# Convolution inputs and decay gates in whole float32, GpSimd out of the first block's splits, and modulation sums moved later

## The chip, the cores and the metric

The kernel runs on one NeuronCore of a Trainium2 chip. The metric is the device time of one execution in microseconds (us); lower is better. TensorE multiplies, VectorE (DVE) and ScalarE (ACT) do elementwise work, GpSimd (POOL) does elementwise work on SBUF, and SyncE (SP) issues most of the transfers.

## The reference, cut to what matters

Two transformer blocks over 256 tokens of width 1024, all in float32. The first block has chunked attention and a gated delta rule side by side, then a feed-forward layer; the second has retention, differential attention and a mixture of 32 experts. The change is in the first block:

```
u = rms_norm(h, mix_norm_gain);  proj = u @ w_in
aq, ak, av, dqkv, dgate, da, db = split(proj)
o_att = rms_norm(chunked_rel_attention(aq, ak, av))
dqkv = causal_short_conv(dqkv)               # 3 x 512 columns: q, k, v of the delta rule
log_decay = -exp(a_log) * softplus(da + dt_bias);  beta = sigmoid(db)
o_dn = rms_norm(gated_delta_rule(dq, dk, dv, log_decay, beta)) * silu(dgate)
h = h + concat(o_att, o_dn) @ w_out
h = h + square(relu(rms_norm(h) @ w_ff1)) @ w_ff2
```

The second block begins with `mod = silu(c) @ w_ada + b_ada`, six vectors of 1024 that scale and shift its norms.

## The kernel before, in words

Most products are made of three passes. Weights come from HBM as float32 tiles `raw` (128 x 2048, 1 MB, a ring of four buffers). `split` cuts a 128 x 1024 piece in two: ScalarE casts it to a rounded high part `hi` (L144), and VectorE or GpSimd subtracts to get the low part `lo` (L145). The numbers in the tuple `POOL` are the splits, counted in the order in which they are written, that GpSimd gets. The activations are kept in the same way as `xh` and `xl`. `gemm_t` then does hi times xh, hi times xl and lo times xh, with the weights stationary and 256 columns moving (L168 to L170); `gemm_b` has the activations stationary and 512 columns moving (L197 to L199). These operands are fp32r; the other products of the kernel have whole float32 operands.

The first block is written as pieces of work. First come the decay gates (`ab_load`, `ab_gemm`, L374 to L376), `conv(1)` (the keys: one `gemm_t` of 512 columns, then the four-tap convolution on VectorE, L325, and SiLU, L328 and L329), `decays`, `l2(1)` and `gram`. Then `level(l, t)` for l = 0 to 6 and two halves t solves the triangular system of the delta rule step by step: GpSimd masks (B, L509), TensorE multiplies (w, L520), ScalarE copies (Ws, L522), TensorE multiplies (u, L527), VectorE subtracts (U, L528). The remaining work is the list `todo`: the convolutions of queries and values, the attention products `qk_gemm`, `v_gemm`, the `head`s, the gate product `gate_gemm`. `ORDER` holds for each entry of the list the level behind which it is written. Behind level 7 comes `scan` (a chain of small products, L533, each waiting for the one before), and at the end `dn_out` and the output product.

A scheduler moves instructions on each engine within what the data allow, by the order in which they are written, so work that is written later fills waits of earlier work. What each engine gets is fixed when the program is built, and each engine works strictly in that order.

`fill` advances the modulation sums: six generators `ada(i)` of four steps each. A step loads 1 MB of `w_ada_2` into the same ring `raw` and adds two 128 x 1024 products on VectorE (L836). `FILL` says how many steps are taken where: five in the first block and 16 in the feed-forward layer; `fill(99)` in the second block takes the last three. The end of the kernel, the experts, streams their weights from HBM.

Of the kernel before, what the change touches and what calls it, by code (L numbers as in the profile page):

```python
# [23 lines left out]
PI_LO = 3.1415925  # L24
FILL = ((0, 0, 0, 0, 0, 0, 1, 2, 2, 0), (1, 1, 1, 1, 0, 1, 1, 1, 1, 1, 1, 1, 1, 1, 1, 2))
NRAW = 4
CHECK = 7
NRAW2B = 2
NRAW2C = 1
ORDER = (1, 2, 2, 6, 6, 6, 7.1, 6.9, 7.9, 6, 6, 6, 8, 8, 8, 8, 8, 8, 8, 8, 8)  # L30
POOL = (1, 5, 8, 9, 11, 13, 14, 21, 24, 25, 30, 31, 32, 33, 36, 37, 38, 40, 42, 48, 60, 83, 104, 106, 117, 140, 144, 152, 155, 158, 186, 187)
TI = 1
# [59 lines left out]
class Build:  # L92
# [66 lines left out]
    def gemm_t(self, W, c0, xt, bank=None):  # L159
# [11 lines left out]
        return [b.rearrange("p (c s) -> p c s", c=2) for b in banks]  # L171

    def gemm_b(self, W, c0, xt, outer=0, halves=(0, 1), bank=None, hook=None):


        nc = self.nc
        xh, xl = xt
        banks = [(bank or self.acc)() for _ in range(2)]
        ps = self.pieces(W, c0, halves)
        def steps():  # L180
            n = 4 * len(halves) - outer
            for _ in range(n):
                p = next(ps)
                for t in range(2):
                    yield t, p
            rest = list(ps)
            for t in range(2):
                for i, p in enumerate(rest):
                    if t == 1 and hook:
                        hook(i, banks)  # L190
                    yield t, p

        k0, k1 = halves[0] * 4, halves[-1] * 4 + 3
        for t, (k, hi, lo) in steps():
            ts = slice(t * 128, (t + 1) * 128)
            o = banks[t]
            nc.tensor.matmul(o, xh[:, k, ts], hi, start=(k == k0), stop=False)  # L197
# [42 lines left out]

    def part_T(self, src, t, k0, gains, xt, bank=None):
# [11 lines left out]
        f = self.t(self.sm, [128, 4, 128], "pf")  # L253
# [38 lines left out]
    def block1(self, x, ctx):  # L292
        nc, d = self.nc, self.d
        T = self.t
# [4 lines left out]
        ss = T(self.sm, [128, 2, 2], "ss")  # L299
        xt = self.xt()  # L300
        for half in range(2):
            for t in range(2):
                self.part_T(x[:, t, half * 512:(half + 1) * 512], t, 4 * half, mix, xt)
        cb = T(p1, [128, 8 * 128], "cb")
# [6 lines left out]
        def conv(s):  # L311
            banks = self.gemm_t(W, 1536 + 512 * s, xt)
            ct = T(p1, [128, 4, 256], f"cT{s}")
# [51 lines left out]
        def ab_load():  # L365
            rawab = T(self.raw, [128, 8, 128], "raw")
            nc.sync.dma_start(rawab, W[:, 3464:3592].rearrange("(k p) c -> p k c", p=128))
            return self.split(rawab.rearrange("p k c -> p (k c)"))

        def ab_gemm(hi, lo):  # L370
            pab = self.mis()
            for k in range(8):
                w = slice(k * 128, (k + 1) * 128)
                nc.tensor.matmul(pab[:, :256], hi[:, w], xt[0][:, k, :], start=(k == 0), stop=False)  # L374
                nc.tensor.matmul(pab[:, :256], hi[:, w], xt[1][:, k, :], start=False, stop=False)
                nc.tensor.matmul(pab[:, :256], lo[:, w], xt[0][:, k, :], start=False, stop=(k == 7))  # L376
            abT = T(p1, [128, 256], "abT")
# [311 lines left out]
        nc.vector.tensor_scalar(rh, r, 0.5, None, op0=OP.mult)  # L689
        ab = ab_gemm(*ab)  # L690
        self.modulation()
# [13 lines left out]
        for t in range(2):  # L705
            gram(t)
        ct = self.xt()
        todo = [lambda: conv(0), lambda: l2(0), lambda: [intra(t) for t in range(2)],
                lambda: qk_gemm(0), lambda: self.fill(FILL[0][7]), lambda: qk_gemm(1), lambda: self.fill(FILL[0][8]), v_gemm, qk_norm,
                lambda: conv(2), lambda: [values(t) for t in range(2)], lambda: self.fill(FILL[0][9])]  # L710
        todo += [lambda h=h: head(h) for h in range(8)]
        todo += [gate_gemm]

        def steps(l):
            for a, i in sorted((a, i) for i, a in enumerate(ORDER)):
                if l <= a < l + 1:
                    todo[i]()

        for l in range(7):
            for t in range(2):  # L720
                level(l, t)
            self.fill(FILL[0][l])
            steps(l)
# [5 lines left out]
        steps(8)  # L729
        dn_out()  # L730
        for t in range(2):
            self.part_T(odn[t], t, 4, gc, ct, self.acc)
        out = [self.gemm_b(d["w_out"][0], half * 512, ct, halves=(1,)) for half in range(2)]
        ra = att_rms()
# [14 lines left out]
    def ffn(self, x, zt, ss, ctx):  # L749
# [9 lines left out]
        def up(s):  # L759
            banks = self.gemm_t(d["w_ff1"][0], 512 * s, zt, bank=self.mis)  # L760
            self.fill(FILL[1][2 * s])
            zh = T(p2, [128, 2, 512], "zh", F32R)
# [11 lines left out]
        for s in range(8):  # L774
# [6 lines left out]
            for half in range(2):  # L781
# [3 lines left out]
                for kk in range(2):  # L785
                    pcs.append((half * 2 + kk, raw[:, kk, :]))
            self.fill(FILL[1][2 * s + 1])
            if s < 7:
# [129 lines left out]
    def block2(self, x, ss, inner, outer):  # L918
# [70 lines left out]
        for s in range(2):  # L989
            banks = self.gemm_b(W, 2048 + 512 * s, xt)  # L990
            for t in range(2):
                cs = slice(s * 512, (s + 1) * 512)
# [14 lines left out]
        dq.append(roped(3584, dqa[:, 4:8, :]))  # L1007
        dk = [roped(4096 + 512 * s, dka[:, 4 * s:4 * s + 4, :]) for s in range(2)]
        dv = tokens(5120, 2, "rv")
# [602 lines left out]
    def run(self):  # L1612
        x = self.setup()
        dense = ExitStack()
        self.sps, self.nsplit, self.total = [self.sp] * 3 + [self.pool("sp1", 1, ctx=dense, side="right")], 0, 0
        with ExitStack() as c:
            zt, ss = self.block1(x, c)
        dense.close()
        if self.stop <= 1:
# [59 lines left out]
```

## Time and profile before

| what | value |
|---|---|
| median of 3 runs | 1209.8 us (1206.2 to 1212.64) |
| the profiled execution | 1207.75 us, span 1205.9 us |
| mean granted TensorE clock | 0.974 of 2.4 GHz |
| busy over the span | TensorE 94%, VectorE 48%, ScalarE 34%, GpSimd 18% |
| first block | from 0 to about 226 us |
| feed-forward layer, second block up to the experts | about 226 to 410, 410 to 726 us |
| experts | about 726 us to the end |

The profile calls the engines PE, DVE, ACT, POOL and SP. A row of the timeline is one instruction or a run of like ones: start, duration, engine, line, output <- inputs, count; the bracket behind it is the idle time of the engine before it and what ended it. Matmuls overlap, so what one of them costs in a stream is the distance of two starts. A product with float32 operands on both sides stands in the trace as two records (a row of x2 is one such instruction).

### The profile page before, as it was taken

The numbers are of one execution on the slowest core, as the hardware profiler recorded it, in microseconds if no ns is written. First come the engines' busy times: TensorE is split into PE (matmuls) and PEld (weight loads), VectorE is DVE, ScalarE is ACT, GpSimd is POOL, SyncE is SP. The second block draws the span as 40 slices with busy tenths as digits, with TensorE's granted clock in tenths as the row PEclk, the third lists the DMA queues.
The fourth block names the chain that finished last, engine by engine and source line by source line (L and its number), as shares of the span: only waits on it lengthen the run. The fifth ranks groups of instructions, "written<-read, shape, count | busy, mean of one in ns | idle before, by whom it ended". The sixth has DMA issues, their size and how long they took to land. (4 is left out here: it accounts for less than half of the span.)

```text
span 1205.9 us, 16461 instructions
## 1 busy us (share of the span) xinstructions
PE 1130.5 (94%) x6638; PEld 810.5 (67%) x6639; DVE 576.6 (48%) x863; ACT 406.0 (34%) x692; POOL 220.6 (18%) x149
## 2 busy tenths in 40 slices
PE   6789799999999999999899989999999799999997
PEld 6768676899899798998899975434343344343443
DVE  5994845786666684788565652111111111120112
ACT  5534344545444445534654441111010011110112
POOL 2472641622010121532220210000000000000011
PEclk9989897999999999999999998999999899999999
DMA  8442531788686746657458585999999999999991
GB/s 300 140 139 72 175 113 51 281 301 283 231 298 240 263 154 185 199 162 258 140 151 292 191 283 217 419 418 415 419 417 415 417 418 415 417 418 416 416 402 62
DMA packets 95728, 331.67 MB, mean 275 GB/s; under 512 B 6528, under 2 KB 11280, under 8 KB 79648
## 3 DMA queue, kind: packets, MB, share of 16 engines
q1 hardware_dynamic: 93152, 327.70, 72.7%
q10 hardware_dynamic: 2448, 2.79, 0.7%
q8 instruction: 53, 0.87, 0.3%
q14 instruction: 27, 0.22, 0.0%
q0 software_dynamic: 48, 0.08, 0.0%
HBM read 329.50 MB, written 1.05 MB: 274 GB/s over the span
## 5 line engine op out<-in xcount | busy, mean ns | idle before, releaser
L144 ACT CAST hi<-raw 128x1024 fp32r<-128x1024 f32 x189 | 197.2, 1046 | 219.2 <-PE acc L169 88.0
L145 DVE TENSOR_TENSOR lo<-raw,hi 128x1024 fp32r<-128x1024 f32 x157 | 210.5, 1350 | 92.6 <-ACT hi L144 90.3
L169 PE MATMUL acc<-xl,hi 128*128 128x256 f32 x544 | 155.2, 285 | 0.9 <-DVE xl L938 0.8
L168 PE MATMUL acc<-xh,hi 128*128 128x256 f32 x544 | 155.8, 287 | 0.0
L170 PE MATMUL acc<-xh,lo 128*128 128x256 f32 x544 | 154.5, 284 | 0.3 <-POOL lo L145 0.3
L169 PEld LDWEIGHTS acc<-xl,hi 128*128 128x128 f32 x544 | 105.0, 193 | 1.4 <-DVE xl L938 1.3
L168 PEld LDWEIGHTS acc<-xh,hi 128*128 128x128 f32 x544 | 105.1, 193 | 0.2
L170 PEld LDWEIGHTS acc<-xh,lo 128*128 128x128 f32 x544 | 104.6, 192 | 0.6 <-POOL lo L145 0.5
L145 POOL TENSOR_TENSOR lo<-raw,hi 128x1024 fp32r<-128x1024 f32 x32 | 80.8, 2530 | 101.0 <-ACT hi L144 100.1
L1422 PE MATMUL mis<-raw,xh 128*64 128x512 f32 x328 | 98.3, 595 | 0.0
L197 PE MATMUL acc<-hi,xh 128*128 128x512 f32 x208 | 86.5, 417 | 0.0
L1413 POOL TENSOR_TENSOR early<-early,x 128x512 f32<-128x512 f32 x4 | 5.0, 1275 | 444.8 <-DVE early L1412 444.8
L198 PE MATMUL acc<-lo,xh 128*128 128x512 f32 x208 | 85.1, 409 | 0.0
L199 PE MATMUL acc<-hi,xl 128*128 128x512 f32 x208 | 84.9, 408 | 0.0
L1467 DVE TENSOR_TENSOR xh<-mis,xh 128x512 fp32r<-128x512 f32 x30 | 20.5, 691 | 115.1 <-ACT xh L1466 114.9
L168 PE MATMUL mis<-xh,hi 128*128 128x256 f32 x256 | 72.6, 284 | 0.0
L170 PE MATMUL mis<-xh,lo 128*128 128x256 f32 x256 | 72.5, 283 | 0.0
L169 PE MATMUL mis<-xl,hi 128*128 128x256 f32 x256 | 72.5, 283 | 0.0
L1433 DVE SCALAR_TENSOR_TENSOR pf<-pf,mis 128x512 f32<-128x512 f32 x16 | 11.0, 688 | 119.6 <-ACT pf L1432 119.6
L836 DVE SCALAR_TENSOR_TENSOR ada<-raw,sc,ada 128x1024 f32<-128x1024 f32 x42 | 61.6, 1467 | 6.8 <-DMA raw<-in_w_ada 6.3
L1422 PE MATMUL mis<-early,xh 128*64 128x512 f32 x256 | 62.9, 595 | 0.0
L1422 PEld LDWEIGHTS mis<-raw,xh 128*64 128x64 f32 x328 | 29.6, 137 | 46.4 <-issue 45.2
(463 smaller groups left out, 2112.1 us busy)
## 6 DMA issues: line engine op xcount, KB each, us to landing
raw<-in_w_in SPq DMA_DIRECT2D x46, 1024.0 KB, 5.4
raw<-in_w_ff SPq DMA_DIRECT2D x32, 1024.0 KB, 5.9
raw<-in_w_exp_up SPq DMA_DIRECT2D x26, 1024.0 KB, 15.0
raw<-in_w_ada SPq DMA_DIRECT2D x24, 1024.0 KB, 6.3
early<-in_w_exp_gate SPq DMA_DIRECT2D x22, 1024.0 KB, 12.6
raw<-in_w_exp_gate SPq DMA_DIRECT2D x15, 1024.0 KB, 17.4
hi<-in_w_exp_up SPq DMA_DIRECT2D x26, 512.0 KB, 13.9
lo<-in_w_exp_up SPq DMA_DIRECT2D x26, 512.0 KB, 12.6
```

The lines of the kernel that those rows point to most:

```text
L144: nc.scalar.copy(hi, raw)
L145: (nc.gpsimd if self.total in POOL else nc.vector).tensor_sub(lo, raw, hi.bitcast(F32))
L168: nc.tensor.matmul(o, hi[:, w], xh[:, k, :], start=(k == 0 and cb % 2 == 0), stop=False, skip_group_check=True)
L169: nc.tensor.matmul(o, hi[:, w], xl[:, k, :], start=False, stop=False, skip_group_check=True)
L170: nc.tensor.matmul(o, lo[:, w], xh[:, k, :], start=False, stop=(k == 7), skip_group_check=True)
L197: nc.tensor.matmul(o, xh[:, k, ts], hi, start=(k == k0), stop=False)
L198: nc.tensor.matmul(o, xh[:, k, ts], lo, start=False, stop=False)
L199: nc.tensor.matmul(o, xl[:, k, ts], hi, start=False, stop=(k == k1))
L836: nc.vector.scalar_tensor_tensor(a, raw[:, kk, :], self.sc[:, k:k + 1], a, op0=OP.mult, op1=OP.add)
L1422: nc.tensor.matmul(o[i * 64:(i + 1) * 64, :], xg[:, k, j % 2 * 128 + i * 64:j % 2 * 128 + (i + 1) * 64], raws[i][kk // 2][:, kk % 2 * 512: ...
L1433: nc.vector.scalar_tensor_tensor(th, th, 1.0, pgt, op0=OP.add, op1=OP.mult)
L1467: nc.vector.tensor_sub(yp[:, 1, c, :], py[c], yp[:, 0, c, :].bitcast(F32))
```

## The change

Three edits and what follows from them. (1) `conv` and `ab_gemm` multiply `raw` by a new tile `xf`, the unrounded activations, in one float32 pass (`gemm_f`); 13 splits (12 of the three convolutions, one of the gates) fall away. (2) `POOL` no longer names a split of the first block: 15 of its 37 splits were GpSimd's, and all 24 that are left are VectorE's. Behind the first block it names the same splits as before, their numbers moved by 13. (3) The five steps of `fill` in the first block move to the second: behind each `gemm_b` of `tokens` and of the retention gates, and once ahead of `dk`. Besides, `ORDER` and a new tuple `OUTS` write the gate product ahead of `scan`, and `dn_out` and the output product's delta-rule half between the heads; the first block's hi and lo have three buffers each in place of four.

```
-FILL = ((0, 0, 0, 0, 0, 0, 1, 2, 2, 0), (1, 1, 1, 1, 0, 1, 1, 1, 1, 1, 1, 1, 1, 1, 1, 2))
+FILL = (1, 1, 1, 1, 0, 1, 1, 1, 1, 1, 1, 1, 1, 1, 1, 2)
-ORDER = (1, 2, 2, 6, 6, 6, 7.1, 6.9, 7.9, 6, 6, 6, 8, 8, 8, 8, 8, 8, 8, 8, 8)
-POOL = (1, 5, 8, 9, 11, 13, 14, 21, 24, 25, 30, 31, 32, 33, 36, 37, 38, 40, 42, 48, 60, 83, 104, 106, 117, 140, 144, 152, 155, 158, 186, 187)
+ORDER = (1, 2, 2, 6, 6, 6.8, 7.9, 6, 6.7, 8.1, 8.2, 8.3, 8.4, 8.6, 8.7, 8.9, 8.95, 6.6)
+OUTS = (8.5, 8.65, 8.8)
+POOL = (24, 25, 27, 29, 35, 47, 70, 91, 93, 104, 127, 131, 139, 142, 145, 173, 174)
...
+    def gemm_f(self, W, c0, xf):
...
+        banks = [self.acc() for _ in range(2)]
+        for half in range(2):
+            raw = self.t(self.raw, [128, 4, 512], "raw")
+            nc.sync.dma_start(raw, W[half * 512:(half + 1) * 512, c0:c0 + 512].rearrange("(k p) c -> p k c", p=128))
+            for kk in range(4):
+                k = half * 4 + kk
+                for cb in range(4):
+                    nc.tensor.matmul(banks[cb // 2][:, (cb % 2) * 256:(cb % 2 + 1) * 256], raw[:, kk, cb * 128:(cb + 1) * 128], xf[:, k, :],
+                                     start=(k == 0 and cb % 2 == 0), stop=(k == 7), skip_group_check=True)
...
         def conv(s):
-            banks = self.gemm_t(W, 1536 + 512 * s, xt)
+            banks = self.gemm_f(W, 1536 + 512 * s, xf)
...
             for k in range(8):
-                w = slice(k * 128, (k + 1) * 128)
-                nc.tensor.matmul(pab[:, :256], hi[:, w], xt[0][:, k, :], start=(k == 0), stop=False)
-                nc.tensor.matmul(pab[:, :256], hi[:, w], xt[1][:, k, :], start=False, stop=False)
-                nc.tensor.matmul(pab[:, :256], lo[:, w], xt[0][:, k, :], start=False, stop=(k == 7))
+                nc.tensor.matmul(pab[:, :256], raw[:, k, :], xf[:, k, :], start=(k == 0), stop=(k == 7))
...
         todo = [lambda: conv(0), lambda: l2(0), lambda: [intra(t) for t in range(2)],
-                lambda: qk_gemm(0), lambda: self.fill(FILL[0][7]), lambda: qk_gemm(1), lambda: self.fill(FILL[0][8]), v_gemm, qk_norm,
-                lambda: conv(2), lambda: [values(t) for t in range(2)], lambda: self.fill(FILL[0][9])]
+                lambda: qk_gemm(0), lambda: qk_gemm(1), v_gemm, qk_norm,
+                lambda: conv(2), lambda: [values(t) for t in range(2)]]
         todo += [lambda h=h: head(h) for h in range(8)]
         todo += [gate_gemm]
+        out = []
+
+        def dn_turn():
+            dn_out()
+            for t in range(2):
+                self.part_T(odn[t], t, 4, gc, ct, self.acc)
+
+        todo += [dn_turn] + [lambda half=half: out.append(self.gemm_b(d["w_out"][0], half * 512, ct, halves=(1,))) for half in range(2)]
...
             for s in range(n):
                 banks = self.gemm_b(W, c0 + 512 * s, xt)
+                self.fill()
```

Two places on VectorE and one on TensorE show how the order moves. On VectorE, between the two halves of the keys' squared sums (`ssd`) and their scaling (`qk`), stood before:

```order
L351 TENSOR_SCALAR ssd_88_441<-ssd_88_441 128x4
L836 SCALAR_TENSOR_TENSOR ada_962<-raw_963,sc_95,ada_962 128x1024
L318 TENSOR_TENSOR pre_675<-acc_556,rrow_178 128x2x256
L145 TENSOR_TENSOR lo_988<-raw_969,hi_987 128x1024
L351 TENSOR_SCALAR ssd_88_441<-ssd_88_441 128x4
L325 SCALAR_TENSOR_TENSOR cT_129_674<-pre_675,cw_224,cT_129_674 128x256
L359 TENSOR_TENSOR qk_93_461<-qk_93_461,rdd_87_440 128x512
L325 SCALAR_TENSOR_TENSOR cT_129_674<-pre_675,cw_224,cT_129_674 128x256 x4
```

and at the same place in the changed kernel stands:

```order
L367 TENSOR_SCALAR ssd_75_335<-ssd_75_335 128x4
L146 TENSOR_TENSOR lo_797<-raw_778,hi_796 128x1024
L146 TENSOR_TENSOR lo_815<-raw_812,hi_814 128x1024
L367 TENSOR_SCALAR ssd_75_335<-ssd_75_335 128x4
L375 TENSOR_TENSOR qk_80_355<-qk_80_355,rdd_74_334 128x512
L334 TENSOR_TENSOR pre_489<-acc_450,rrow_168 128x2x256
L460 SCALAR_TENSOR_TENSOR L_296<-mis_378,beta_140,L_296 128x128 x4
```

The modulation product is gone, a second low part stands in its place, and the convolution of the queries (`cT`) has moved behind the gram product (L460, before L447). On VectorE in levels 1 and 2 (the four subtractions from U), before:

```order
L528 TENSOR_TENSOR U_507<-U_507,mis_535 128x128x2
L325 SCALAR_TENSOR_TENSOR cT_129_674<-pre_689,cw_224,cT_129_674 128x256
L145 TENSOR_TENSOR lo_1022<-raw_1003,hi_1021 128x1024
L836 SCALAR_TENSOR_TENSOR ada_962<-raw_1047,sc_95,ada_962 128x1024
L528 TENSOR_TENSOR U_518<-U_518,mis_550 128x128x2
L329 SCALAR_TENSOR_TENSOR cT_129_674<-sq_700,cT_129_674 128x512
L836 SCALAR_TENSOR_TENSOR ada_962<-raw_1047,sc_95,ada_962 128x1024
L836 SCALAR_TENSOR_TENSOR ada_962<-raw_1051,sc_95,ada_962 128x1024
L528 TENSOR_TENSOR U_507<-U_507,mis_718 128x64x4
L836 SCALAR_TENSOR_TENSOR ada_962<-raw_1051,sc_95,ada_962 128x1024
L528 TENSOR_TENSOR U_518<-U_518,mis_739 128x64x4
```

and now:

```order
L541 TENSOR_TENSOR U_401<-U_401,mis_429 128x128x2
L341 SCALAR_TENSOR_TENSOR cT_108_488<-pre_489,cw_198,cT_108_488 128x256
L341 SCALAR_TENSOR_TENSOR cT_108_488<-pre_503,cw_198,cT_108_488 128x256 x2
L345 SCALAR_TENSOR_TENSOR cT_108_488<-sq_500,cT_108_488 128x512
L341 SCALAR_TENSOR_TENSOR cT_108_488<-pre_503,cw_198,cT_108_488 128x256 x3
L541 TENSOR_TENSOR U_412<-U_412,mis_444 128x128x2
L341 SCALAR_TENSOR_TENSOR cT_108_488<-pre_503,cw_198,cT_108_488 128x256
L146 TENSOR_TENSOR lo_831<-raw_812,hi_830 128x1024
L345 SCALAR_TENSOR_TENSOR cT_108_488<-sq_514,cT_108_488 128x512
L541 TENSOR_TENSOR U_401<-U_401,mis_532 128x64x4
L541 TENSOR_TENSOR U_412<-U_412,mis_553 128x64x4
```

Four modulation products between the subtractions are gone, and convolution steps stand there that were done earlier before. On TensorE at the scan (L533, now L546), before:

```order
L533 MATMUL mis_1422<-vb_1287,U_507 128x128 x4
L198 MATMUL acc_1692<-lo_1697,xh_106 128x512
L199 MATMUL acc_1692<-hi_1696,xl_107 128x512
L197 MATMUL acc_1693<-hi_1696,xh_106 128x512
L198 MATMUL acc_1693<-lo_1697,xh_106 128x512
L199 MATMUL acc_1693<-hi_1696,xl_107 128x512
L197 MATMUL acc_1692<-hi_1696,xh_106 128x512
L533 MATMUL mis_1429<-D_1421,kt_147 128x128 x4
L198 MATMUL acc_1692<-lo_1697,xh_106 128x512
```

and now:

```order
L214 MATMUL acc_1094<-hi_1147,xl_104 128x512
L601 MATMUL mis_1171<-ca_84,qk_179_846 128x128 x4
L601 MATMUL mis_1178<-ca_84,qk_181_851 128x128 x4
L601 MATMUL mis_1186<-ca_84,qk_195_926 128x128 x4
L601 MATMUL mis_1193<-ca_84,qk_197_931 128x128 x4
L546 MATMUL mis_1200<-vb_1084,U_401 128x128 x4
L546 MATMUL mis_1207<-D_1199,kt_141 128x128 x4
L546 MATMUL mis_1214<-s_248_1206,cT_56_243 128x128 x4
L546 MATMUL mis_1222<-Ws_1213,U_412 128x128 x4
L546 MATMUL mis_1228<-D_1199,LT_297 128x128 x4
```

The products that stood between the scan's steps now stand ahead of it, and nothing stands between the steps.

## Rows read from the trace of the kernel before

**Rows 1.** The page: mean GB/s that the transfers moved, in 40 equal slices.

```profile
GB/s 300 140 139 72 175 113 51 281 301 283 231 298 240 263 154 185 199 162 258 140 151 292 191 283 217 419 418 415 419 417 415 417 418 415 417 418 416 416 402 62
```

**Rows 2.** The page's costliest groups: out<-in xcount, busy us, mean ns, idle before.

```profile
L145 DVE TENSOR_TENSOR lo<-raw,hi 128x1024 fp32r<-128x1024 f32 x157 | 210.5, 1350 | 92.6 <-ACT hi L144 90.3
...
L145 POOL TENSOR_TENSOR lo<-raw,hi 128x1024 fp32r<-128x1024 f32 x32 | 80.8, 2530 | 101.0 <-ACT hi L144 100.1
...
L836 DVE SCALAR_TENSOR_TENSOR ada<-raw,sc,ada 128x1024 f32<-128x1024 f32 x42 | 61.6, 1467 | 6.8 <-DMA raw<-in_w_ada 6.3
```

**Rows 3.** Stretches: length, busy us and instructions per engine, granted clock, DMA share, GB/s.

```profile
120.00:140.00 20.00, 13.83 (x94) 12.53 (x92) 19.35 (x17) 8.07 (x11) 17.89 (x8) 0.91 0.50 162
140.00:160.00 20.00, 18.88 (x104) 16.48 (x105) 10.74 (x15) 7.98 (x12) 0.62 (x2) 0.83 0.51 179
...
540.00:560.00 20.00, 20.00 (x117) 17.76 (x116) 17.28 (x16) 8.42 (x9) 8.38 (x5) 1.00 0.63 196
```

**Rows 4.** Timeline of TensorE at the end of the keys' product.

```profile
31.04 0.28 PE L170 MATMUL acc<-xh,lo 128*128 128x256 f32 x1
31.16 0.28 PE L417 MATMUL mis<-g,cb 128*128 128x4 f32 x2
```

**Rows 5.** Timeline of TensorE in retention: whole float32, 256 columns.

```profile
469.37 0.59 PE L971 MATMUL mis<-ga 128*128 128x256 f32 x2
469.80 0.38 PE L972 MATMUL mis<-ga 128*128 128x128 f32 x2
```

**Rows 6.** Timeline of TensorE where the decay gates begin.

```profile
12.29 0.39 PE L374 MATMUL mis<-xh,hi 128*128 128x256 f32 x1 [2.58 <-ACT hi L144]
...
13.55 0.46 PE L376 MATMUL mis<-xh,lo 128*128 128x256 f32 x1 [0.76 <-DVE lo L145]
...
17.90 0.39 PE L170 MATMUL acc<-xh,lo 128*128 128x256 f32 x1 [0.31 <-POOL lo L145]
```

**Rows 7.** Timeline of VectorE from 30 to 60 us.

```profile
32.73 6.65 DVE L325 SCALAR_TENSOR_TENSOR cT<-pre,cw,cT 128x256 f32<-128x256 f32 x12
...
46.27 1.27 DVE L836 SCALAR_TENSOR_TENSOR ada<-raw,sc,ada 128x1024 f32<-128x1024 f32 x1
...
48.68 1.95 DVE L145 TENSOR_TENSOR lo<-raw,hi 128x1024 fp32r<-128x1024 f32 x1
50.55 1.00 DVE L351 TENSOR_SCALAR ssd<-ssd 128x4 f32<-128x4 f32 x1
...
52.84 2.84 DVE L359 TENSOR_TENSOR qk<-qk,rdd 128x512 f32<-128x512 f32 x1 [0.90 <-POOL rdd L352]
```

**Rows 8.** Timeline of VectorE in levels 1 and 2.

```profile
64.88 6.86 DVE L325 SCALAR_TENSOR_TENSOR cT<-pre,cw,cT 128x256 f32<-128x256 f32 x4
...
73.08 3.39 DVE L145 TENSOR_TENSOR lo<-raw,hi 128x1024 fp32r<-128x1024 f32 x1
76.39 2.28 DVE L836 SCALAR_TENSOR_TENSOR ada<-raw,sc,ada 128x1024 f32<-128x1024 f32 x1
78.59 0.41 DVE L528 TENSOR_TENSOR U<-U,mis 128x256 f32<-128x256 f32 x1
...
79.53 3.48 DVE L836 SCALAR_TENSOR_TENSOR ada<-raw,sc,ada 128x1024 f32<-128x1024 f32 x2
...
83.26 1.98 DVE L836 SCALAR_TENSOR_TENSOR ada<-raw,sc,ada 128x1024 f32<-128x1024 f32 x1
```

**Rows 9.** Timeline of TensorE from 140 to 163 us.

```profile
141.12 1.11 PE L466 MATMUL mis<-ca,cT 128*128 128x128 f32 x4 [7.29 <-DVE cT L329]
...
156.20 1.05 PE L533 MATMUL mis<-D,kt 128*128 128x128 f32 x8
...
158.02 1.07 PE L533 MATMUL mis<-s,cT 128*128 128x128 f32 x8
...
161.23 1.16 PE L533 MATMUL mis<-Ws,U 128*128 128x128 f32 x8 [0.51 <-POOL Ws L546]
162.23 1.06 PE L533 MATMUL mis<-D,LT 128*128 128x128 f32 x8
```

More of the change, by code (lines that the diff above doesn't have):

```diff
@@ L171, in gemm_t @@
         return [b.rearrange("p (c s) -> p c s", c=2) for b in banks]
+    def gemm_f(self, W, c0, xf):
+        nc = self.nc
+        banks = [self.acc() for _ in range(2)]
[7 more added lines that the diff above has]
+                                     start=(k == 0 and cb % 2 == 0), stop=(k == 7), skip_group_check=True)
+        return [b.rearrange("p (c s) -> p c s", c=2) for b in banks]
     def gemm_b(self, W, c0, xt, outer=0, halves=(0, 1), bank=None, hook=None):
@@ L239, in xt, with part_T @@
         return (self.t(self.xtp, [128, 8, 256], "xh", F32R), self.t(self.xtp, [128, 8, 256], "xl", F32R))
-    def part_T(self, src, t, k0, gains, xt, bank=None):
+    def part_T(self, src, t, k0, gains, xt, bank=None, whole=None):
         nc = self.nc
@@ L252, in part_T @@
             return
-        f = self.t(self.sm, [128, 4, 128], "pf")
+        f = self.t(self.sm, [128, 4, 128], "pf") if whole is None else whole[:, k0:k0 + 4, ts]
         nc.vector.tensor_mul(f, ps, gains[:, k0:k0 + 4, None].to_broadcast([128, 4, 128]))
@@ L300, in block1 @@
         xt = self.xt()
+        xf = T(p1, [128, 8, 256], "xf")
         for half in range(2):
             for t in range(2):
-                self.part_T(x[:, t, half * 512:(half + 1) * 512], t, 4 * half, mix, xt)
+                self.part_T(x[:, t, half * 512:(half + 1) * 512], t, 4 * half, mix, xt, whole=xf)
         cb = T(p1, [128, 8 * 128], "cb")
@@ L367, in ab_load, with ab_gemm @@
             nc.sync.dma_start(rawab, W[:, 3464:3592].rearrange("(k p) c -> p k c", p=128))
-            return self.split(rawab.rearrange("p k c -> p (k c)"))
-        def ab_gemm(hi, lo):
+            return rawab
+        def ab_gemm(raw):
             pab = self.mis()
             for k in range(8):
-                w = slice(k * 128, (k + 1) * 128)
-                nc.tensor.matmul(pab[:, :256], hi[:, w], xt[0][:, k, :], start=(k == 0), stop=False)
-                nc.tensor.matmul(pab[:, :256], hi[:, w], xt[1][:, k, :], start=False, stop=False)
-                nc.tensor.matmul(pab[:, :256], lo[:, w], xt[0][:, k, :], start=False, stop=(k == 7))
+                nc.tensor.matmul(pab[:, :256], raw[:, k, :], xf[:, k, :], start=(k == 0), stop=(k == 7))
             abT = T(p1, [128, 256], "abT")
@@ L689, in block1 @@
         nc.vector.tensor_scalar(rh, r, 0.5, None, op0=OP.mult)
-        ab = ab_gemm(*ab)
+        ab = ab_gemm(ab)
         self.modulation()
@@ L708, in block1 @@
         todo = [lambda: conv(0), lambda: l2(0), lambda: [intra(t) for t in range(2)],
-                lambda: qk_gemm(0), lambda: self.fill(FILL[0][7]), lambda: qk_gemm(1), lambda: self.fill(FILL[0][8]), v_gemm, qk_norm,
-                lambda: conv(2), lambda: [values(t) for t in range(2)], lambda: self.fill(FILL[0][9])]
+                lambda: qk_gemm(0), lambda: qk_gemm(1), v_gemm, qk_norm,
+                lambda: conv(2), lambda: [values(t) for t in range(2)]]
         todo += [lambda h=h: head(h) for h in range(8)]
         todo += [gate_gemm]
+        out = []
[4 more added lines that the diff above has]
+        todo += [dn_turn] + [lambda half=half: out.append(self.gemm_b(d["w_out"][0], half * 512, ct, halves=(1,))) for half in range(2)]
         def steps(l):
-            for a, i in sorted((a, i) for i, a in enumerate(ORDER)):
+            for a, i in sorted((a, i) for i, a in enumerate(ORDER + OUTS)):
                 if l <= a < l + 1:
@@ L721, in block1 @@
                 level(l, t)
-            self.fill(FILL[0][l])
             steps(l)
@@ L729, in block1 @@
         steps(8)
[L730 to L733, printed above, removed]
         ra = att_rms()
@@ L760, in up @@
             banks = self.gemm_t(d["w_ff1"][0], 512 * s, zt, bank=self.mis)
-            self.fill(FILL[1][2 * s])
+            self.fill(FILL[2 * s])
             zh = T(p2, [128, 2, 512], "zh", F32R)
@@ L786, in ffn @@
                     pcs.append((half * 2 + kk, raw[:, kk, :]))
-            self.fill(FILL[1][2 * s + 1])
+            self.fill(FILL[2 * s + 1])
             if s < 7:
@@ L990, in block2 @@
             banks = self.gemm_b(W, 2048 + 512 * s, xt)
+            self.fill()
             for t in range(2):
@@ L1007, in block2 @@
         dq.append(roped(3584, dqa[:, 4:8, :]))
+        self.fill()
         dk = [roped(4096 + 512 * s, dka[:, 4 * s:4 * s + 4, :]) for s in range(2)]
@@ L1614, in run @@
         dense = ExitStack()
-        self.sps, self.nsplit, self.total = [self.sp] * 3 + [self.pool("sp1", 1, ctx=dense, side="right")], 0, 0
+        self.sps, self.nsplit, self.total = [self.sp] * 3, 0, 0
         with ExitStack() as c:
             zt, ss = self.block1(x, c)
-        dense.close()
         if self.stop <= 1:
```

## The prediction

> **What bounds the kernel now.** I read the page's bytes per slice first. From slice 26 on, about 750 us, the transfers run at 415 to 419 GB/s up to the last two slices [rows 1]: there the experts wait for weights. In the first block, up to 226 us, the same row says 51 to 300, so transfers do not bound it. What comes ahead of the experts is one sequence in time, and where TensorE is busy without a gap, as in 540 to 560 us (20.00 of 20, [rows 3]), nothing can be caught up. So I carry every microsecond won or lost in the first block to the end one to one.
>
> Second, the groups by cost: a low part takes VectorE 1.35 us in the mean and GpSimd 2.53, a modulation product 1.467 [rows 2]. Third, the first block in stretches and timelines. From 120 to 140 us VectorE is busy 19.35 of 20 us and GpSimd 17.89, while TensorE has 13.83 [rows 3], and TensorE then waits 7.29 us for the values' convolution [rows 9]. The same instruction forms are much longer here than elsewhere: a low part 1.95 and 3.39, a modulation product 2.28 and 1.98 against 1.27, four convolution taps 6.86 against twelve in 6.65 [rows 7, 8]. VectorE, slowed beside GpSimd, bounds about half of this block, and the waits for one another the rest.
>
> **The change part by part.** Stretches of the first block are costed apart, each by what ends its wait.
>
> *Float32 products.* In a stream one fp32r product of 256 columns takes 0.12 us (31.04 to 31.16, [rows 4]), a whole float32 one of the same size 0.43 (469.37 to 469.80, [rows 5]). One convolution was 32 x 3 x 0.12 = 11.5 us and becomes 32 x 0.43 = 13.8: +2.3. The gates were 24 x 0.12 = 2.9 and become 8 x 0.43 = 3.4: +0.6. The keys' +2.3 and the gates' +0.6 lie on the path; so does the values' +2.3 (below). The queries' +2.3 lies in levels 1 and 2, where TensorE waits for VectorE; with that cover gone it costs 2.3.
>
> *To 31 us.* The gates waited 2.58 us for ScalarE's cast, then 0.76 and 0.31 for low parts [rows 6]. The casts are gone, and what is awaited now is the weights' landing, later than the end of the work before by something between 0 and 2.58; I take a gain of half, 1.3, and of both other waits, 1.1. Against +2.9 that leaves +0.5. A low part (1.35) may stand between the keys' two scalings on VectorE: 0 to 1.35, I take 0.5, since VectorE has waits there. Together **+1.0** (bounds -1.1 to +3.2).
>
> *31 to 60 us, the keys' chain to the gram product.* VectorE is the path. A modulation product goes (-1.27). One low part of 1.95 becomes two of 1.35 (+0.75). `qk` took 2.84 [rows 7]; an undisturbed one of half the width takes 0.41 [rows 8], so 0.8 without GpSimd's low part beside it: -2.0, or nothing if GpSimd's other work disturbs it as much. `ssd`, four elements wide, took 1.00; 0.41 is its upper bound: -0.6. The first tap ahead of `qk` (6.65/12 = 0.55) moves behind gram: -0.55. Sum **-3.7** (with `qk` unhelped -1.7; with `ssd` free -4.1).
>
> *Levels 1 and 2.* Between the four subtractions from U stood one low part of 3.39 and four modulation products, 2.28 + 3.48 + 1.98 = 7.74 [rows 8]. Now one low part of 1.35 stands there: -2.04 - 7.74 = -9.8. But taps that were done earlier have moved in, six more of them and about a scaling (0.8). At 0.55 that is +4.1, a net gain of 5.7. With half of them beside GpSimd's masks at 6.86/4 = 1.72, it is 6 x 1.13 + 0.8 = 7.6, a net gain of 2.2. GpSimd keeps its masks, so I take the middle: **-4.0**.
>
> The shared access of VectorE and GpSimd is what these sums rest on. The Trainium skill (SBUF — State Buffer, Who interferes with whom) says that a VectorE instruction with two SBUF inputs contends with a GpSimd instruction that reads SBUF, and that the holder keeps the shared port pair for its whole instruction. The trace agrees with 3.39 against 1.35 for the same form. By the rule alone all 15 x 2.53 = 38 us of GpSimd's low parts would be the outer limit of what VectorE gets back; the masks, which it would also let block, stay.
>
> *Levels 3 to 6, then to 140 us.* The list is the same work, and TensorE's own. At the end the wait of 7.29 us [rows 9] is VectorE's lateness with the values. VectorE keeps about as many low parts as before (24 for 22 in the whole block), loses GpSimd's 17.89 us beside it, but gets the gate product's low parts ahead of the scan, the last of them behind the convolution. Between no gain and all of it, I take about half: -3.5. The clock was granted at 0.91 in 120 to 140 and 0.83 in 140 to 160 us [rows 3]: the latter is 0.17 x 20 = 3.4 us behind full speed, following that wait. With a shorter wait I take half, -1.7. The values' product adds +2.3.
>
> *The scan.* Before, products of the gates stood between its steps and TensorE idled only 0.51 us there. Now the steps stand bare. A step through ScalarE's copy starts 1.82 us after the one before (156.20 to 158.02), one through VectorE and GpSimd 3.21 (158.02 to 161.23), and the product itself takes about 1.0 [rows 9]. Three copies and one longer hand-over: 3 x 0.77 + 2.16 - 0.51 = +4.0 (bounds +3, were the old starts held back by the filler, to +5.5 at half clock). The filler is not lost: it stands ahead, so the work is done, but the gap is new. Scan and stretch before it: 2.3 - 3.5 - 1.7 + 4.0 = **+1.1** (bounds -5.4 to +7.8).
>
> *Heads and output.* The delta-rule half of the output now fills the later heads as the gate product did, and the first heads lose theirs: I cost it at 0. If the first two heads idle as the scan does, +4 more.
>
> *Moved modulation and buffers.* Five steps, ten VectorE products of 1.467 = 14.7 us and 5 MB, go to the second block. In 540 to 560 us VectorE has 17.28 of 20 busy, TensorE 20.00, the transfers a share of 0.63 [rows 3]; over 316 us of that block the cover is ample, so 0; where it fails, in stretches like this one, a step of 2.9 us meets 2.7 free. Three buffers in place of four: 0, since 13 splits less use them.
>
> Sum: 1.0 - 3.7 - 4.0 + 1.1 = **-5.6**. The profiled execution took 1207.75 us, 2.05 below the median; -5.6 gives **1202**.
>
> **The rivals.** (a) As summed: 1202, own range 1197 to 1207.
> (b) The waits vanish wholly: -7.3 and -3.4 instead of -3.5 and -1.7, -5.7 in the levels: 5.5 + 1.7 = 7.2 more, and some of the heads' waits: 1193. For it speaks that GpSimd's 17.89 us lies on just that stretch; against it, the low parts that VectorE takes over.
> (c) The gain is given back: either the first heads stand bare (+4) or the values' wait stays with its clock (3.5 + 1.7 = +5.2), 1206 to 1207, or both, 1211; for the case I take 1208, nothing that can be measured. For it speaks that the masks still slow VectorE in the levels.
> (d) Slower, by TensorE's clock. After the 7.29 us wait the granted clock was 0.83 over the next 20 us [rows 3], with 1.2 GHz in part of it. If the bare scan and first heads bring such a fall and hold it, a stretch like 140 to 160 us, 18.88 us busy at 0.83 or 15.7 at full speed, would take 31.3 at half: +12.4. From 1202 the loss decides at 14 us, about 22 us of time more at half clock than before; scan and two or three heads are 25 to 30 us: 1218. Against it: the heads carry dense products of the output half again. The Trainium skill (TensorE: Matmul & The Clock Gate, HAM oscillation — how this bites in real kernels) says that idle gaps between bursts throttle the clock anew each time and that the penalty is paid each time; the trace agrees in that the low clock of [rows 3] follows a wait, and by that rule alone rival (d) would be the outcome.
> (e) The second block is bound by VectorE in a few stretches, or its weights wait behind the moved loads in the ring of raw tiles: half of the 14.7 us shows, 1202 + 7 = 1209, all of it 1217.
>
> **How the numbers follow.** A measurement of this kernel can tell about 0.5% from no change, 6 us: below 1203.8 is faster, above 1215.8 slower. Chances: (a) 0.49, (b) 0.13, (c) 0.21, (d) 0.11, (e) 0.06. Of (a) some two thirds lie below 1203.8, with (b) and a little of (c): faster 0.49; (d) and a third of (e): slower 0.13; the rest 0.38. The bounds of the terms add to -16 on the one side (1191) and +7 on the other (1215). I take 1190 to 1213: (d), a third of (e) and a little of (b) stay outside.
>
> **What would show it.** Right: no `ada` row and no GpSimd low part before 226 us; the gram product some 3 us earlier; the levels' U subtractions close together by about 4 us; the wait for the values' convolution well below 7 us; gaps of 0.8 and 2.2 us between the bare scan products; the end of the first block about 220 us; the second block's length unchanged, TensorE 20 of 20. Wrong: low parts and taps still at 2 us or more beside the masks; a granted clock near 0.5 from the scan through the heads; the values' wait still there; float32 products in other than 0.43 us each; a second block longer than before.

## The result and the profile after

The changed kernel takes 1218.83 us in the median of seven runs, the kernel before 1211.68 beside it: ratio 1.0066, 95% interval 1.0039 to 1.0093. It is slower by 0.7%, where 1202 was forecast. The profiled executions have spans of 1217.2 and 1205.9 us; these 11.3 us are more than the medians' 7.2, because the one profiled of before is among its fastest. The gain came, and somewhat larger than forecast, up to 90 us; it was given back at three later places:

| stretch, by TensorE's timeline | before, us | after, us | difference |
|---|---|---|---|
| start to the first product behind the levels | 98.95 | 89.56 | -9.4 |
| from there to the scan's first product | 54.97 | 59.38 | +4.4 |
| to the turning of the first pair of heads | 23.73 | 34.02 | +10.3 |
| to the feed-forward layer's first product | 48.62 | 43.09 | -5.5 |
| that layer, to the first product behind it | 190.01 | 199.89 | +9.9 |
| the rest of the span | 789.6 | 791.3 | +1.6 |

The layer ends at 416.3 us in the kernel before, not at about 410. The last row is the TensorE product of one modulation sum, 1.84 us, which stood at 150.21 us before and now stands in the second block.

The stretches of the changed kernel, in the columns of [rows 3], answer to those of before:

```profile
120.00:140.00 20.00, 20.00 (x95) 16.84 (x94) 14.49 (x24) 9.02 (x13) 4.48 (x5) 1.00 0.62 203
140.00:160.00 20.00, 15.51 (x83) 13.54 (x82) 5.60 (x5) 8.09 (x13) 1.26 (x1) 0.83 0.32 106
160.00:180.00 20.00, 15.27 (x58) 10.79 (x57) 9.18 (x27) 4.37 (x13) 5.96 (x6) 0.59 0.03 7
...
236.00:246.00 10.00, 7.36 (x49) 7.36 (x50) 8.45 (x14) 1.77 (x3) 0.35 (x2) 0.71 0.81 304
540.00:560.00 20.00, 20.00 (x169) 20.00 (x168) 18.30 (x18) 7.34 (x7) 9.11 (x5) 1.00 0.51 159
```

From 120 to 140 us VectorE no longer bounds (14.49 for 19.35) and TensorE is full: the 7.29 us wait of [rows 9] is gone. From 160 to 180 us TensorE is idle a quarter of the time and runs at 0.59 of its clock, between its levels of 1.2 and 2.4 GHz. VectorE's timeline from 44 to 72 us, for [rows 7, 8]:

```profile
43.99 2.35 DVE L146 TENSOR_TENSOR lo<-raw,hi 128x1024 fp32r<-128x1024 f32 x2
46.71 0.17 DVE L367 TENSOR_SCALAR ssd<-ssd 128x4 f32<-128x4 f32 x1 [0.36 <-ACT sq L363]
50.47 0.69 DVE L375 TENSOR_TENSOR qk<-qk,rdd 128x512 f32<-128x512 f32 x1 [3.58 <-POOL rdd L368]
...
64.04 2.28 DVE L341 SCALAR_TENSOR_TENSOR cT<-pre,cw,cT 128x256 f32<-128x256 f32 x3
...
69.49 1.21 DVE L146 TENSOR_TENSOR lo<-raw,hi 128x1024 fp32r<-128x1024 f32 x1
...
71.75 0.42 DVE L541 TENSOR_TENSOR U<-U,mis 128x256 f32<-128x256 f32 x1 [0.45 <-PE mis L540]
```

The short durations are back: `qk` 0.69 for 2.84, a low part 1.2 for 1.95 and 3.39. Then TensorE's timeline at the scan and the first heads:

```profile
151.69 1.16 PE L546 MATMUL mis<-D,kt 128*128 128x128 f32 x8 [1.69 <-ACT D L554]
153.52 2.07 PE L546 MATMUL mis<-s,cT 128*128 128x128 f32 x8 [0.68 <-ACT s L556]
157.72 2.08 PE L546 MATMUL mis<-Ws,U 128*128 128x128 f32 x8 [2.12 <-POOL Ws L559]
...
168.00 0.48 PE L645 MATMUL mis<-ca,pre 128*128 128x128 f32 x1 [2.07 <-ACT pre L642]
...
171.74 0.90 PE L263 MATMUL acc<-ca,B 128*128 128x128 f32 x3 [1.92 <-DVE B L690]
```

TensorE waits between the scan's steps, and the same products take 2.07 us behind these waits that took 1.07 in [rows 9], which is half clock. Last, the entry of the feed-forward layer, on VectorE, TensorE and SyncE of the changed kernel:

```profile
234.98 2.40 DVE L852 SCALAR_TENSOR_TENSOR ada<-raw,sc,ada 128x1024 f32<-128x1024 f32 x1 [5.34 <-DMA raw<-in_w_ada]
237.31 1.28 DVE L271 TENSOR_TENSOR xl<-pf,xh 128x512 fp32r<-128x512 f32 x2
```

```profile
238.64 0.58 PE L170 MATMUL mis<-xl,hi 128*128 128x256 f32 x1 [5.66 <-DVE xl L271]
```

```profile
227.59 0.37 SPq L846 DMA_DIRECT2D raw<-in_w_ada  x1
```

and, of the kernel before, on SyncE:

```profile
224.21 0.37 SPq L830 DMA_DIRECT2D raw<-in_w_ada  x1
```

TensorE waits for `xl`; `xl` is ready to be made but stands on VectorE behind a modulation product, whose weights were asked for at 227.59, 1.5 us after the layer's first product (226.05). In the kernel before the same load went out at 224.21, 2.1 us ahead of that product (226.27). The kernel before has no wait in this layer and runs it at full clock. In the changed kernel there is a second wait at the layer's last modulation sum:

```profile
413.20 1.92 PE L857 MATMUL mis<-ones,ada 128*128 128x1 f32 x16 [0.79 <-DVE ada L852]
```

Of the layer's 9.9 us more, 5.66 and 0.79 are these two waits, and about 3.3 are the half clock that follows them, over 6.7 us of products. The sums' own products add nothing: there are four of them in the layer in either kernel.

### The profile page after: what moved, and what is told of

It reads as the page before. It is cut to its first block, busy times and chain, and to the rows that moved or that the text cites. A ratio compares the mean times of both kernels' runs of the same rounds, so it can differ in the third digit from the quotient of the medians.

```text
span 1217.2 us, 16206 instructions
## 1 busy us (share of the span) xinstructions
PE 1139.1 (94%) x6534; PEld 812.2 (67%) x6535; DVE 548.8 (45%) x865; ACT 393.7 (32%) x679; POOL 174.6 (14%) x134
## 5 line engine op out<-in xcount | busy, mean ns | idle before, releaser
L145 ACT CAST hi<-raw 128x1024 fp32r<-128x1024 f32 x176 | 183.8, 1047 | 214.6 <-PE acc L170 76.5
L146 DVE TENSOR_TENSOR lo<-raw,hi 128x1024 fp32r<-128x1024 f32 x159 | 203.6, 1289 | 86.1 <-ACT hi L145 85.5
L170 PE MATMUL acc<-xl,hi 128*128 128x256 f32 x448 | 127.3, 284 | 0.9 <-DVE xl L954 0.8
L169 PE MATMUL acc<-xh,hi 128*128 128x256 f32 x448 | 127.6, 285 | 0.0
L171 PE MATMUL acc<-xh,lo 128*128 128x256 f32 x448 | 127.0, 284 | 0.0
L170 PEld LDWEIGHTS acc<-xl,hi 128*128 128x128 f32 x448 | 86.0, 192 | 1.4 <-DVE xl L954 1.3
L169 PEld LDWEIGHTS acc<-xh,hi 128*128 128x128 f32 x448 | 85.9, 192 | 0.1
L171 PEld LDWEIGHTS acc<-xh,lo 128*128 128x128 f32 x448 | 85.9, 192 | 0.1
L852 DVE SCALAR_TENSOR_TENSOR ada<-raw,sc,ada 128x1024 f32<-128x1024 f32 x42 | 56.0, 1332 | 16.7 <-DMA raw<-in_w_ada 16.1
L1441 PE MATMUL mis<-hi,xh 128*64 128x512 f32 x152 | 56.7, 597 | 0.0
```

Of the source, the lines that this page charges most:

```text
L145: nc.scalar.copy(hi, raw)
L146: (nc.gpsimd if self.total in POOL else nc.vector).tensor_sub(lo, raw, hi.bitcast(F32))
L169: nc.tensor.matmul(o, hi[:, w], xh[:, k, :], start=(k == 0 and cb % 2 == 0), stop=False, skip_group_check=True)
L170: nc.tensor.matmul(o, hi[:, w], xl[:, k, :], start=False, stop=False, skip_group_check=True)
L171: nc.tensor.matmul(o, lo[:, w], xh[:, k, :], start=False, stop=(k == 7), skip_group_check=True)
L852: nc.vector.scalar_tensor_tensor(a, raw[:, kk, :], self.sc[:, k:k + 1], a, op0=OP.mult, op1=OP.add)
```

## The experiments

Ratios are to the kernel before, run on the same chip. The groups of runs were on different chips, so a difference between two ratios is less certain than each of them.

**Take the late step out.** The second step moves one place on.

```
-FILL = (1, 1, 1, 1, 0, 1, ...
+FILL = (1, 1, 0, 1, 1, 1, ...
```

> The changed kernel, but the second modulation step of the feed-forward layer, whose first product TensorE waited for behind VectorE at its entry (5.66 us, then a clock of 0.71 for 10 us), is taken one place later. Theory A (that one product, stuck in VectorE's order on a late load, makes the loss at the entry): the wait is below 1 us, and the time is 7 to 8 us less than the changed kernel, 0.999 to 1.001 of the kernel before. Rival B (the entry waits for late weights in any case, whatever VectorE holds): another wait of 3 us or more stands there, and the ratio stays at 1.004 or above.

1.0098 (1.0064 to 1.0133): no gain. The 5.66 us are gone, but the layer still takes 199.4 us: at 274.40 TensorE waits 2.48 us for a later modulation sum, and the granted clock is 0.85 from 260 to 280 us. The wait moved along. Theory A fell; the lateness is not one product's.

**Filler behind the heads, as before.** Gate product and output half are written behind the heads again.

```
-ORDER = (..., 8.9, 8.95, 6.6)
-OUTS = (8.5, 8.65, 8.8)
+ORDER = (..., 8.9, 8.95, 8.97)
+OUTS = (8.98, 8.985, 8.99)
```

> The changed kernel with the gate product written behind the heads, and the delta-rule half of the output product behind it, as in the kernel before. Theory A (the bare scan and the first heads give back what the levels gain: 0.59 of the clock in 160 to 180 us): from the scan's start to the end of the heads it takes 5 to 9 us less than in the changed kernel, the granted clock over it is above 0.8, and the ratio to the kernel before falls by 0.004 to 0.007 to about 1.000. Rival B (the product has to be done anyhow, the filler only changes places): the end of the first block stays within 2 us, the ratio at 1.005 or above.

0.9893 (0.9863 to 0.9922), 21 us less than the changed kernel: theory A's direction, and three times its size. Half of it is the scan's earlier start, which A did not have. The scan begins at 137.99 for 148.94, the first pair of heads is turned 24.8 us behind that for 34.0, the feed-forward layer begins at 204.19 for 226.05.

**Float32 products alone, and three buffers alone**, each in the kernel before.

```
+self.sps, self.nsplit, self.total = [self.sp] * 3, 0, 0
```

> The kernel before with the float32 products alone (and three buffers, for which the unrounded activations leave room); GpSimd keeps its low parts, modulation and filler stay in their old places. Theory A (float32 products cost their 2.3 us each for two convolutions, and fewer casts and low parts give some of it back): 0.998 to 1.002 by the products, and up to 1.006 if the missing fourth buffer stalls the entry of the feed-forward layer. Rival B (the products alone make the whole loss): 1.006 or more with no wait at that entry.

> The kernel before with three buffers for high and low parts in the first block in place of four, and nothing else changed. Theory A (with three buffers the casts ahead of the feed-forward layer wait for TensorE one piece more, the ring of raw tiles comes free 3 us later, and the modulation load lands late): a wait of 2 us or more at the entry of the feed-forward layer, 1.003 to 1.007. Rival B (the fourth buffer hardly matters): within 1.002, no such wait.

Three buffers alone: 1.0146 (1.0118 to 1.0173), 17 us, twice what was expected; the scan begins at 160.37 for 153.92, and the feed-forward layer takes 200.6 us for 190.0. Float32 products with three buffers: 1.0016 (0.9997 to 1.0036). So the products, with 13 casts and low parts less, are worth about 15 us against the same buffers: the levels end at 89.30 for 99.21.

**Gate product between scan and heads; output half behind, gate ahead.** The changed kernel with one of the two numbers put back.

```
+ORDER = (..., 8.95, 8.05)
```

> The changed kernel with the gate product written between the scan and the heads, the delta-rule half as in the changed kernel. Theory A (the bare scan starts the loss: after its gaps TensorE runs at half clock through the first heads): with products of the gates between the scan's steps the granted clock of 160 to 180 us rises from 0.59 to above 0.9 and most of the 21 us between the changed kernel and the one with the filler behind come back: 0.990 to 0.996 of the kernel before. Rival B (the heads without filler are the loss, not the scan): 1.001 or more, since the first heads stay as bare as they are.

```
+OUTS = (8.98, 8.985, 8.99)
```

> The changed kernel with the delta-rule half of the output product written behind the heads, the gate product ahead of the scan as in the changed kernel. Theory A (the scan's missing filler makes the loss, the place of the output product hardly any): 1.004 to 1.009, scan and clock as in the changed kernel. Rival B (the output half that is written between the heads delays them): 0.997 or less.

1.0017 (0.9999 to 1.0036) and 1.0029 (1.0014 to 1.0043): 6 and 4 us. In the first run rival B's number came, but not by its reason; in the second neither theory's number did. With the gate product ahead of the heads the scan is filled and begins at 137.88, but the first pair is turned 33.2 us behind it, as late as with a bare scan: the products that rank ahead of the heads hold the heads up (7 us of them stand between the scan and the first head). Only both pieces behind the heads bring the whole gain.

**Repeated products in the gaps; the gate product twice.** Both add work that is thrown away.

```
+            again(U[0], vb[0], 6)
...
+            again(kt, vn, 2)
...
+            again(cT[1][:, :, 128:256], s1, 8)
```

> The changed kernel with products repeated, their results unused, in the gaps of the bare scan (6, 2 and 8 of 128x128) and of the first two heads (4 of 64x256 each). They compute nothing that is needed. Theory A (the clock: gaps bring the half speed, and the half speed costs more than the gaps): 160 to 180 us runs at 0.85 or more in place of 0.59 and the time falls by 4 to 9 us, 0.999 to 1.003 of the kernel before. Rival B (the waits themselves and the chain of scan and heads are the loss, the clock only follows): no gain or a loss, 1.006 to 1.010.

```
-OUTS = (8.5, 8.65, 8.8)
+OUTS = (8.5, 8.65, 8.8, 8.45)
...
+        todo += [lambda: self.gemm_b(W, 3072, xt)]
```

> The changed kernel with the gate product computed a second time, its result unused: the first stays ahead of the scan, the second stands between the steps of the scan and in the first heads just where the filler stood in the kernel with the filler behind. It adds 48 products of 0.23 us, 11 us of TensorE, 2 MB of loads and four splits. Theory A (the bare waits and the half clock behind them cost time beyond what the filler hides): the clock of 150 to 180 us is 1.00 and the feed-forward layer begins 6 to 11 us earlier than in the changed kernel although TensorE has 11 us more to do; 0.997 to 1.002 of the kernel before. Rival B (the filler was worth only the work that it hid): the second product is hidden for nothing, no gain, 1.005 to 1.010.

Repeats: 1.0060 (1.0045 to 1.0074), no gain that can be told. The gate product twice: 1.0040 (1.0022 to 1.0058), some 3 us less than the changed kernel with 11 us more for TensorE; the two intervals overlap. The stretches of the first, then of the second:

```profile
140.00:160.00 20.00, 19.43 (x122) 17.08 (x121) 8.73 (x10) 9.75 (x14) 0.62 (x1) 1.00 0.47 163
160.00:180.00 20.00, 17.35 (x78) 12.16 (x77) 7.90 (x24) 3.04 (x10) 6.60 (x7) 0.74 0.04 11
```

```profile
140.00:160.00 20.00, 19.39 (x120) 16.58 (x119) 8.11 (x7) 9.29 (x14) 1.87 (x2) 1.00 0.34 122
160.00:180.00 20.00, 18.66 (x90) 12.74 (x89) 14.18 (x39) 8.78 (x21) 5.37 (x6) 0.98 0.31 102
```

The repeats hold the clock through the scan and lose it in the heads (0.74); from the scan's first product to the first pair it is 32.1 us. The second gate product keeps 1.00 and 0.98, and this stretch takes 26.0 us in place of 34.0. Useless work thus saves 8 us there.

In the scan 3.6 of them are the clock. The changed kernel's bare scan stands unaltered in four profiled kernels (the changed one, the one without the early step, the one with only the output half behind, and the late buffer in the changed kernel, below). From its first to its last product it waits the same 4.5 us in each and takes 15.03, 13.05, 13.04 and 11.41 us, at a granted clock of 0.66, 0.87, 0.87 and 1.00. With the second gate product between its steps it takes 11.44. The changed kernel and the late buffer:

```profile
148.94:163.97 15.03, 10.54 (x58) 9.87 (x56) 3.20 (x4) 3.87 (x7) 2.30 (x2) 0.66 0.17 64
```

```profile
146.90:158.31 11.41, 6.93 (x57) 6.36 (x56) 2.61 (x3) 3.85 (x7) 1.96 (x2) 1.00 0.32 95
```

So the scan's waits cost no time by themselves; half clock does. The other 4.4 us lie in the first heads, where the order differs as well: eight transposes of the delta rule's output (L263) stand ahead of the turned pair in the changed kernel, three with the second gate product. The run with the gate product behind the scan has all eight and takes 14.7 us from the first head's first product to the turned pair, at a clock of 0.81, for 18.8 at 0.57. That speaks for the clock here too, but filler also fills 2 us of its waits, so the share of the heads is argued and not shown.

From the pair to the feed-forward layer 5.5 us are lost again (48.6 for 43.1; clock 0.74 from 200 to 220 us). The layer begins at 223.28, 2.8 us ahead of the changed kernel where theory A had 6 to 11, and the run without the early step, whose first block is the changed kernel's, begins it at 223.97. The run's whole time decides for neither theory.

**GpSimd's low parts, and the five modulation steps, given back** to the kernel with the filler behind.

```
+POOL = (0, 2, 4, 5, 8, 11, 12, 17, 18, 19, 20, 23, 24, ...
```

> The kernel with gate and output half behind the heads (0.989 of the kernel before), with the 12 low parts of the first block that GpSimd had before and that still exist given back to it. Theory A (GpSimd's low parts slow VectorE in the chain to the gram product and in levels 1 and 2): the gram product and the levels end 3 to 6 us later, 0.992 to 0.996. Rival B (the modulation sums and the casts were the whole burden, GpSimd's low parts are hidden): within 2 us of the kernel without them, 0.987 to 0.991.

```
+            if l == 6:
+                self.fill()
...
+                lambda: [qk_gemm(0), self.fill(2)], lambda: qk_gemm(1), v_gemm, lambda: [self.fill(2), qk_norm()],
```

> The kernel with gate and output half behind the heads (0.989 of the kernel before), with the five modulation steps taken in the first block again, at their old places. Theory A (the levels' gain comes from the splits that float32 products make needless; the modulation sums cost little there): the levels end within 2 us of the kernel without them, 0.988 to 0.993. Rival B (the prediction's: modulation products between the levels' subtractions cost 4 to 8 us): the levels end 4 us later or more, 0.994 to 0.998.

GpSimd's low parts: 0.9996 (0.9978 to 1.0014), so without them some 12 us are saved, more than either theory had, but not where A said: the levels end at 88.45 for 89.28. They cost at the values' convolution and in the heads (from the first pair to the feed-forward layer 51.8 us for 41.4). In the heads most of the cost is the clock: TensorE is busy 47.83 us at 0.80 there, for 39.42 at 1.00; why it falls stays open. VectorE with GpSimd's low parts, GpSimd beside it, and VectorE without them:

```profile
128.57 5.11 DVE L341 SCALAR_TENSOR_TENSOR cT<-pre,cw,cT 128x256 f32<-128x256 f32 x2
```

```profile
127.33 6.06 POOL L146 TENSOR_TENSOR lo<-raw,hi 128x1024 fp32r<-128x1024 f32 x2 [4.04 <-ACT hi L145]
```

```profile
129.57 0.88 DVE L341 SCALAR_TENSOR_TENSOR cT<-pre,cw,cT 128x256 f32<-128x256 f32 x2
```

The same two taps: 5.11 us beside two subtractions of GpSimd, 0.88 alone. The Trainium skill (SBUF — State Buffer, Who interferes with whom) says that such a VectorE instruction, with two SBUF inputs, contends with a GpSimd one that reads SBUF; the trace agrees, with these numbers. The modulation steps: 0.9941 (0.9921 to 0.9962), about 6 us; the levels end 4.7 us later (93.96), which is rival B, and 4.3 us of it come back behind the feed-forward layer (310.8 us to the experts for 315.1).

**A fourth buffer from the last convolution on.** The unrounded activations stand in a pool that is closed behind `conv(2)`, and their place becomes the fourth high and low buffer; in the kernel with the filler behind, and in the changed kernel.

```
+        xf = T(self.pool("xfp", 1, ctx=xfc, side="right"), [128, 8, 256], "xf")
...
+        def late():
+            xfc.close()
+            self.sps.append(self.pool("sp1", 1, ctx=self.dense, side="right"))
```

> The kernel with gate and output half behind the heads (0.989 of the kernel before), in which the unrounded activations stand in a buffer of their own that is given up behind the last convolution and becomes the fourth high and low buffer. Theory A (the three buffers make the casts ahead of the feed-forward layer one piece later, so its second modulation load is issued 1.4 to 2.2 us after the first product of that layer where the kernel before had it 2.1 us ahead): the load is issued ahead of the first product, the layer takes 191 to 193 us in place of 197, and the ratio falls to 0.983 to 0.987. Rival B (the layer is longer for another reason): it stays at 196 us or more, the ratio at 0.988 to 0.991.

> The changed kernel with the same fourth buffer from the last convolution on. Theory A (three buffers make the late load): the wait of 5.66 us at the entry of the feed-forward layer is below 1 us, the layer takes 191 to 193 us in place of 199.9, 0.999 to 1.003 of the kernel before. Rival B (the wait there comes from the order of the loads, not from the buffers): the wait stays above 3 us, 1.005 to 1.008.

0.9844 (0.9821 to 0.9868), 1192.18 us, the fastest kernel of this study, and 1.0025 (1.0010 to 1.0039). In the changed kernel with it the load goes out ahead of the layer's first product again; SyncE and TensorE:

```profile
220.29 0.37 SPq L851 DMA_DIRECT2D raw<-in_w_ada  x1
```

```profile
222.91 0.28 PE L169 MATMUL mis<-xh,hi 128*128 128x256 f32 x1
```

The wait at the entry is 1.36 us for 5.66, and the layer takes 194.3 us (194.2 in the other). The buffers make the late load, as theory A has it, but its numbers came only in part: the wait is not below 1 us, and 194 is above its 191 to 193. In the changed kernel with the fourth buffer the layer is 4.3 us longer than in the kernel before: the waits at its entry and at its last modulation sum (1.36 and 0.79), 1.7 of half clock behind the second, and 0.5 that I can't name.

## Why the prediction was wrong

| stretch | forecast, us | measured, us |
|---|---|---|
| to the end of the levels | 1.0 - 3.7 - 4.0 = -6.7 | -9.4 |
| to the scan's first product | 2.3 - 3.5 - 1.7 = -2.9 | +4.4 |
| scan and first pair of heads | +4.0 | +10.3 |
| later heads and output | 0 | -5.5 |
| feed-forward layer | 0 | +9.9 |
| the rest | 0 | +1.6 |
| sum | -5.6 | +11.3 |

The sum was set on one profiled execution; set on the median of 1209.8 it gives 1204. The lower bound of the first term adds up to -0.8, not -1.1. Neither matters beside the steps below.

**What held.** A whole float32 product costs 0.43 us: 32 of them took 13.97. Up to the end of the keys' product +0.7 came, from there to the gram product -5.2 (it begins at 51.77 for 56.29), in the levels -4.9: each term has the right sign, and the second and third are larger than forecast. `qk` and `ssd` shrank as priced. The values' wait vanished, where half was taken. The scan's three waits, 1.69, 0.68 and 2.12, add to 4.5, as worked out.

**The step that failed** is the one at the scan and the heads: "The filler is not lost: it stands ahead, so the work is done, but the gap is new", with +4.0 for the gap, nothing for the work put ahead, and the first heads at 0. TensorE is full ahead of the scan, so the gate product's 48 x 0.23 = 11 us, which had stood in the waits of the scan and the heads, went onto the path: from the levels to the scan it takes 59.4 us, and 48.7 in both runs that write the gate product later. The gap itself costs almost nothing: at full clock the bare scan takes 11.41 us, 11.45 with the filler behind and 10.87 in the kernel before, since the chain sets its length with or without filler. What came with the gap is half clock. Against the kernel with the filler behind, the scan begins 10.95 us later; scan and first pair then take 9.2 us longer, 3.6 in the scan, which is the clock, and 5.7 in the first heads, of which up to 4.4 are the clock by the run with the gate product twice. With 1.4 in the other heads and 0.3 behind them, these make the 21.9 by which the feed-forward layer begins later. Of a thing moved, I had priced the place that it left and not the place that it went to.

**"Three buffers in place of four: 0"** failed too. In the changed kernel the fourth buffer is worth 5 to 6 us (1.0066 to 1.0025), by the layer's entry; in the kernel before, with its 13 splits more, 17.

**Moved modulation at 0** was off by some 4 us: 2.5 at the layer's last sum (the wait of 0.79, which stands only in kernels whose sums were moved, and the half clock behind it) and 1.6 behind the layer. Rival (e) had seen it larger.

**GpSimd's low parts** were priced at the wrong place. I took the stretched rows 30 to 80 us into the block for a cost on the path; with the low parts given back the levels end no later. Of the 17.89 us that GpSimd was busy from 120 to 140 us, low parts were only 6.9. The levels' gain is VectorE's load: with the splits less, it is there when the sums leave (89.28), when GpSimd takes its low parts with the sums in place (89.30) or when both leave VectorE (88.45), and half lost when VectorE has both (93.96).

**Rival (d)**, 1218 at 0.11, gave the time that was measured, by luck for the most part. The clock did fall in the scan and the first heads, to 0.59 over 20 us, worth at most 8 us and not the 14 that (d) needed; 11 more of the 22 are work laid bare, which (d) did not have. And up to the feed-forward layer there was no more half clock than before: the kernel before lost as much around 140 us and in its later heads, and the mean granted clock is 0.92 in both, here of before, then of after:

```profile
0.00:226.27 226.27, 192.90 (x1202) 161.87 (x1204) 158.97 (x268) 102.73 (x201) 98.77 (x72) 0.92 0.44 145
```

```profile
0.00:226.05 226.05, 198.69 (x1083) 162.50 (x1084) 118.32 (x259) 89.74 (x188) 56.06 (x57) 0.92 0.38 122
```

The Trainium skill's rule that gaps bring the throttle back each time (TensorE: Matmul & The Clock Gate, HAM oscillation — how this bites in real kernels) agrees with the 0.59 behind the scan's waits, but not with its "each time": in the late-buffer run the clock stays at 1.00 through the same three waits and falls only in the heads.

Left open: how much of the first heads' 5.7 us is the clock and how much the order, and what makes the clock fall in one execution of the same bare scan and not in another.

## What to carry to other kernels

A product that fills waits is priced by the work that it hides and the clock that it holds, at the place that it leaves, and by whether the engine has room at the place where it goes. Filler has to rank behind the chain that it fills: ahead of it, it delays the chain. A wait in a chain that other engines pace costs nothing by itself; ask whether the chain gets longer. Give up a buffer only after asking which transfer waits for its release, and what stands on an engine behind the instruction that awaits that transfer.

## What was not expected of the hardware

In the run with repeated products the granted clock fell to half without a wait: TensorE was busy without a gap from 71 us on, in the dependent products of the levels and then in a product's stream, and the clock was 0.50 from 96 to 104 us, 1.00 from 110 on. The changed kernel, with the same products there, has 1.00 from 96 to 104 us. This cost that execution about 4 us ahead of all that the run was meant to change.

```profile
80.00:90.00 10.00, 10.00 (x82) 8.75 (x80) 2.93 (x6) 2.84 (x7) 1.56 (x2) 1.00 0.00 0
96.00:104.00 8.00, 8.00 (x44) 6.17 (x44) 1.62 (x4) 2.12 (x4) 1.34 (x2) 0.50 0.31 116
```
